# Score tiles of four levels for two token tiles in a gated linear attention, and its output with the state terms first

## The chip, the core and the metric

The kernel runs on one core of a Trainium2 chip. The time is the device time of one execution in microseconds (us). The engines work side by side, each through its own queue in order: TensorE (PE; its weight loads stand apart as PEld), VectorE (DVE), ScalarE (ACT), GpSimd (POOL), and SyncE (SP), whose queue issues the transfers from DRAM.

## The reference

The program is a block of two layers on 512 latent tokens and 256 context tokens, with 1024 features, and a second block behind it. In each layer three branches run side by side: a gated convolution, an attention and a gated linear attention (GLA). The GLA has four heads with 128 key and 256 value features. Its core, for one direction, is

```python
def _gla_scan(q, k, v, log_a, s0):
    ...
    def step(s, inp):
        qc, kc, vc, ac = inp
        bcum = jnp.cumsum(ac, axis=2)
        o_inter = jnp.einsum('bhtd,bhde->bhte', qc * jnp.exp(bcum), s)
        diff = bcum[:, :, :, None, :] - bcum[:, :, None, :, :]
        decay = jnp.exp(jnp.where(mask[:, :, None], diff, -jnp.inf))
        att = jnp.einsum('bhtd,bhsd,bhtsd->bhts', qc, kc, decay)
        o_intra = jnp.einsum('bhts,bhse->bhte', att, vc)
        b_last = bcum[:, :, -1:, :]
        s_new = jnp.exp(b_last[:, :, 0, :])[..., None] * s + jnp.einsum('bhsd,bhse->bhde', kc * jnp.exp(b_last - bcum), vc)
        return s_new, o_inter + o_intra
```

It runs over the tokens forward and backward, first over the context and from the states reached there over the latents; the two directions are added.

## The kernel before

The kernel works on tiles of 128 tokens. In such a tile the decay between two tokens depends on each feature, so the 128 x 128 square of scores is split into seven levels and a diagonal: at level L the tile falls into blocks of 128 >> L tokens, and the decay between a token of one half of a block and one of the other half is measured from the border between the halves. Each level is then a plain matmul of decayed queries with decayed keys, of which a 0/1 mask (`gm`, 8 x 128 columns) keeps the pairs that belong to that level. The eight masked squares are added into one.

`gla_levels` does this for one head. A *unit* is 256 tokens, two token tiles c = 0, 1. Per level, GpSimd makes four subtractions into a tile x (L946 to L949; the context's and the latents' x share three buffers), ScalarE takes the exponential (L950), VectorE multiplies by queries and keys (L951), and TensorE makes one score matmul for each c (L955). Both c have a score tile of 128 x 1024 columns, with a slot of 128 for each level and the diagonal (L959); there are two such buffers, `sc`. When the diagonal of c is done, VectorE masks its tile in two halves of four slots (L964), adds the four slots of each up (L968), and GpSimd adds the two sums into the square `att` (L973). Then the generator yields 1900.

`gla_out` makes the output of a head: for each of two blocks e of 128 value features, and each token tile i, the queries with the states of the two directions (`S`, forward and backward) and then the values with `att`, all by L994 into one bank `mm`, which has one buffer. ScalarE copies and squares the result.

`gla_main` calls for each head the states (`gla_states`), then the levels in turns with the decay of the next head (`gla_decay`, with the triangular matmul L854), then the output. This runs three times: on the context in layer 0 (one unit for each head), on the latents in layer 0 and on the latents in layer 1 (two units for each head); the context in layer 1 needs only states.

What sets the order around this is a pump. Other work of the layer, above all projections (L274, L276, with weights split in two parts by L253 on ScalarE and L254 on VectorE), is written as generators and put into a queue, the *filler*. Each yield of the GLA's generator names some nanoseconds; scaled (by 1.2 for the latents, 3.0 for the context) they buy that much filler, which is written behind it. Filler for the latents comes from projections, for the context at its end from the modulation: groups of four matmuls (L536) whose weights of 512 KB come by DMA into three buffers `wr`, with two groups of L548 to close. A scheduler then settles each engine's order. There is no filler when the queue is empty.

Of the kernel before, what the change touches and what calls it, by code (L numbers as in the profile page):

```python
# [10 lines left out]
F32 = mybir.dt.float32  # L11
# [3 lines left out]
ALU = mybir.AluOpType  # L15
# [169 lines left out]
class Kern:  # L185
# [745 lines left out]
    def gla_levels(self, G, hd):  # L931
# [3 lines left out]
        for un in range(T // 256):  # L935
            uc = slice(un * 256, (un + 1) * 256)
            sl = [self.sc() for _ in range(2)]
            for L in range(7):
# [13 lines left out]
                yield 1500  # L952
                for c in range(2):
                    cs = slice(c * 128, (c + 1) * 128)
                    nc.tensor.matmul(sl[c][:, L * 128:(L + 1) * 128], x[:, 1, cs], x[:, 0, cs],  # L955
                                     start=True, stop=True)
            for c in range(2):
                cs = slice(un * 256 + c * 128, un * 256 + (c + 1) * 128)
                nc.tensor.matmul(sl[c][:, 896:1024], qk[:, 1, cs], qk[:, 0, cs], start=True, stop=True)  # L959
                att = pool.tile([128, 128], F32, tag="att", name=self.nm("att"), bufs=4)  # L960
                part = None
                for hf in range(2):
                    pr = pool.tile([128, 512], F32, tag="pr", name=self.nm("pr"), bufs=1)
                    nc.vector.tensor_tensor(pr, sl[c][:, hf * 512:(hf + 1) * 512],  # L964
                                            G["gm"][:, 4 * hf:4 * hf + 4, :].rearrange("p a b -> p (a b)"),
                                            op=ALU.mult)
                    o = att if part is None else self.sm2()
                    nc.vector.tensor_reduce(o, pr.rearrange("p (a b) -> p b a", a=4),  # L968
                                            axis=mybir.AxisListType.X, op=ALU.add)
                    if part is None:  # L970
                        part = att
                    else:
                        nc.gpsimd.tensor_tensor(att, att, o, op=ALU.add)  # L973
                G["att"][hd].append(att)
                yield 1900
# [4 lines left out]
    def gla_out(self, G, hd, pump):  # L980
# [4 lines left out]
        for e in range(2):  # L985
# [4 lines left out]
            for i in range(nt):  # L990
                terms = [(S[d][i][:, es], qd[:, d, i * 128:(i + 1) * 128]) for d in range(2) if S[d][i] is not None]
                terms.append((gv[:, i, es], atts[i]))
                for n_, (a, b) in enumerate(terms):
# [1150 lines left out]
```

## Time and profile before

| | us |
|---|---|
| median of three runs | 3627.67 |
| lowest and highest | 3621.95 and 3629.71 |
| the profiled execution | 3630.32 |
| its span, first to last instruction | 3628.5 |
| TensorE busy | 3482.0 |
| VectorE busy | 2087.1 |
| ScalarE busy | 1502.2 |
| GpSimd busy | 457.7 |

The mean granted clock of TensorE is 0.985 of full speed. The span is shared between the instructions of the engines; busy times of different engines overlap, and only what TensorE doesn't do is left for a change that leaves its matmuls alone. A wait is named after the instruction that came last of those waited for. Each f32 matmul stands in the rows as two records (x2). The recorded time of a row with several records starts with the first and ends with the last, and overlaps the row behind it; the pace is read from start to start.

### The profile page before, as it was taken

Reading aid. Unit: us, or ns where it says so; the run is one execution under the profiler, and the core shown is the slowest. Engines: PE = TensorE matmul, PEld = TensorE weight load, DVE = VectorE, ACT = ScalarE, POOL = GpSimd, SP = SyncE. Lnnn points to the kernel's source line nnn. Section 1 sums busy time; section 2 is a strip of 40 time slices with the busy share of each in tenths; the row PEclk is TensorE's granted clock in tenths of the full one; section 3 lists DMA queues with packets and bytes.
Section 4 is the critical chain, followed back from the end, with each engine's and each line's share of the span. In section 5 each row is a group of like instructions: output and inputs, shape, how many; then the busy total and the mean of one; then the engine's idle time right before and its main releaser. Section 6 shows DMA issues by size and latency. Waiting matters only on the chain. (4 is left out here: it accounts for less than half of the span.)

```text
span 3628.5 us, 52736 instructions
## 1 busy us (share of the span) xinstructions
PE 3482.0 (96%) x20382; PEld 2966.3 (82%) x20382; DVE 2087.1 (58%) x4317; ACT 1502.2 (41%) x2574; POOL 457.7 (13%) x802
## 2 busy tenths in 40 slices
PE   7999999999999999999999999999899999989999
PEld 5998888988888878887888887887788687678887
DVE  5755556578545555666755555445576547665342
ACT  4543333445534434444553443222444445533241
POOL 0011211010123340010013332000200000000000
PEclk8999999999999999999999999999999999999999
DMA  6443334531222224532122222323412332232222
GB/s 226 133 145 115 117 119 150 199 112 47 73 83 73 80 92 154 180 124 85 53 72 79 74 85 88 116 99 128 164 59 79 103 107 86 77 110 87 95 99 93
DMA packets 144091, 386.61 MB, mean 107 GB/s; under 512 B 17496, under 2 KB 47456, under 8 KB 143584
## 3 DMA queue, kind: packets, MB, share of 16 engines
q1 hardware_dynamic: 143840, 383.24, 31.9%
q8 instruction: 160, 2.62, 0.3%
q14 instruction: 91, 0.75, 0.1%
HBM read 345.92 MB, written 30.96 MB: 104 GB/s over the span
## 5 line engine op out<-in xcount | busy, mean ns | idle before, releaser
L254 DVE TENSOR_TENSOR wl<-wr,wh 128x1024 fp32r<-128x1024 f32 x522 | 650.1, 1247 | 665.9 <-PE pj L274 325.3
L274 PE MATMUL pj<-h,wh 128*128 128x512 f32 (+1 forms) x2568 | 928.7, 372 | 13.9 <-ACT wh L253 5.5
L276 PE MATMUL pj<-h,wh 128*128 128x512 f32 (+1 forms) x2568 | 910.4, 365 | 0.0
L253 ACT ACTIVATE wh<-wr 128x1024 fp32r<-128x1024 f32 x522 | 550.3, 1057 | 778.1 <-PE pj L276 549.0
L274 PE MATMUL pj<-h,wl 128*128 128x512 f32 (+1 forms) x2568 | 594.2, 367 | 0.0
L274 PEld LDWEIGHTS pj<-h,wh 128*128 128x128 f32 x2568 | 488.6, 191 | 85.5 <-ACT wh L253 8.0
L276 PEld LDWEIGHTS pj<-h,wh 128*128 128x128 f32 x2568 | 488.7, 191 | 63.2 <-issue 0.6
L274 PEld LDWEIGHTS pj<-h,wl 128*128 128x128 f32 x2568 | 434.8, 190 | 68.1 <-issue 1.2
L274 PE MATMUL pj<-uh,wh 128*128 128x256 f32 (+1 forms) x1040 | 324.5, 335 | 17.0 <-ACT uh L258 5.1
L276 PE MATMUL pj<-ul,wh 128*128 128x256 f32 (+1 forms) x1040 | 320.6, 331 | 2.7 <-DVE ul L259 2.6
L274 PEld LDWEIGHTS pj<-uh,wh 128*128 128x128 f32 x1040 | 198.2, 191 | 37.8 <-ACT uh L258 6.5
L276 PEld LDWEIGHTS pj<-ul,wh 128*128 128x128 f32 x1040 | 199.2, 192 | 20.5 <-DVE ul L259 4.5
L274 PE MATMUL pj<-uh,wl 128*128 128x256 f32 (+1 forms) x1040 | 202.4, 333 | 0.0
L951 DVE TENSOR_TENSOR x<-x,qk 128x512 f32<-128x512 f32 x140 | 107.6, 774 | 133.9 <-ACT x L950 133.9
L950 ACT ACTIVATE x<-x 128x512 f32<-128x512 f32 x140 | 88.3, 631 | 230.5 <-POOL x L949 216.4
L320 PE MATMUL pj<-wh,h 128*128 128x256 f32 x608 | 176.7, 291 | 0.9 <-DVE vl L259 0.9
L322 PE MATMUL pj<-wl,h 128*128 128x256 f32 x608 | 174.2, 287 | 1.4 <-DVE wl L254 1.3
L274 PEld LDWEIGHTS pj<-uh,wl 128*128 128x128 f32 x1040 | 160.4, 194 | 15.7
L321 PE MATMUL pj<-wh,h 128*128 128x256 f32 x608 | 173.3, 285 | 0.0
L946 POOL TENSOR_TENSOR x<-bc 128x128 f32<-128x128 f32 x140 | 72.9, 521 | 466.8 <-PE sc L955 465.6
L322 PEld LDWEIGHTS pj<-wl,h 128*128 128x128 f32 x608 | 116.9, 192 | 2.4 <-DVE wl L254 2.0
L320 PEld LDWEIGHTS pj<-wh,h 128*128 128x128 f32 x608 | 117.2, 193 | 1.5 <-DVE vl L259 1.0
(376 smaller groups left out, 5887.6 us busy)
## 6 DMA issues: line engine op xcount, KB each, us to landing
wr<-in_w_br_dram SPq DMA_DIRECT2D x84, 512.0 KB
wr<-in_w_mg_dram SPq DMA_DIRECT2D x72, 512.0 KB
wr<-in_w_ada_dram SPq DMA_DIRECT2D x48, 512.0 KB
wr<-in_w_f_dram SPq DMA_DIRECT2D x45, 512.0 KB
wr<-in_w_o_dram SPq DMA_DIRECT2D x37, 512.0 KB
wr<-in_wt_gv_dram SPq DMA_DIRECT2D x32, 512.0 KB
wr<-in_w_up_dram SPq DMA_DIRECT2D x32, 512.0 KB
wr<-in_w_dn_dram SPq DMA_DIRECT2D x32, 512.0 KB
```

The lines of the kernel that those rows point to most:

```text
L253: self.nc.scalar.activation(hi, raw, AF.Copy)
L254: self.nc.vector.tensor_tensor(lo, raw, hi.bitcast(F32), op=ALU.subtract)
L274: t.matmul(ps[:, :T], c, h[k][0], start=start and n == k == 0, stop=stop and last)
L276: t.matmul(ps[:, :T], c, h[k][1], start=False, stop=False)
L320: t.matmul(ps[:, :256], hh, hi[:, c], start=k == 0, stop=False)
L321: t.matmul(ps[:, :256], hl, hi[:, c], start=False, stop=False)
L322: t.matmul(ps[:, :256], hh, lo[:, c], start=False, stop=k == KT - 1)
L946: nc.gpsimd.tensor_tensor(xv[0][:, :, 0, :], v[1][:, :, 0, :], cm, op=ALU.subtract)
L950: nc.scalar.activation(x, x, AF.Exp)
L951: nc.vector.tensor_tensor(x, x, qk[:, :, uc], op=ALU.mult)
```

## The change

A score tile now holds four levels of both token tiles: 512 columns for c = 0 and 512 for c = 1. The first tile of a unit takes levels 0 to 3, the second takes levels 4 to 6 and the diagonal. `masked(sl, hf)` masks one of them: for each c a product with the mask over 512 columns, a reduction, and for the second tile an addition to the first one's sum, on VectorE where GpSimd did it. It is called behind level 3 for the first tile and behind the diagonal for the second, and yields 1000 after each c, four times a unit where there were two yields of 1900. In the output, all state terms of a bank come first and all `att` terms last, with one start and one stop over the bank. Ahead of the output stands a new yield of 2500. In the changed code the mask's product is L943, the reduction L947, the addition L950, the level's product L966, the score matmul L973, the diagonal L978 and the output L998.

```diff
--- before.py
+++ after.py
@@ -934,7 +934,22 @@
         G["att"][hd] = []
         for un in range(T // 256):
             uc = slice(un * 256, (un + 1) * 256)
-            sl = [self.sc() for _ in range(2)]
+            att = [pool.tile([128, 128], F32, tag="att", name=self.nm("att"), bufs=4) for _ in range(2)]
+
+            def masked(sl, hf):
+
+                for c in range(2):
+                    pr = pool.tile([128, 512], F32, tag="pr", name=self.nm("pr"), bufs=1)
+                    nc.vector.tensor_tensor(pr, sl[:, c * 512:(c + 1) * 512],
+                                            G["gm"][:, 4 * hf:4 * hf + 4, :].rearrange("p a b -> p (a b)"),
+                                            op=ALU.mult)
+                    o = self.sm2() if hf else att[c]
+                    nc.vector.tensor_reduce(o, pr.rearrange("p (a b) -> p b a", a=4),
+                                            axis=mybir.AxisListType.X, op=ALU.add)
+                    if hf:
+                        nc.vector.tensor_tensor(att[c], att[c], o, op=ALU.add)
+                        G["att"][hd].append(att[c])
+                    yield 1000
             for L in range(7):
                 m = 64 >> L
                 x = pool.tile([128, 2, 256], F32, tag="x", name=self.nm("x"), bufs=3)
@@ -950,29 +965,18 @@
                 nc.scalar.activation(x, x, AF.Exp)
                 nc.vector.tensor_tensor(x, x, qk[:, :, uc], op=ALU.mult)
                 yield 1500
+                if L % 4 == 0:
+                    sl = self.sc()
                 for c in range(2):
                     cs = slice(c * 128, (c + 1) * 128)
-                    nc.tensor.matmul(sl[c][:, L * 128:(L + 1) * 128], x[:, 1, cs], x[:, 0, cs],
-                                     start=True, stop=True)
+                    os_ = slice(c * 512 + L % 4 * 128, c * 512 + L % 4 * 128 + 128)
+                    nc.tensor.matmul(sl[:, os_], x[:, 1, cs], x[:, 0, cs], start=True, stop=True)
+                if L == 3:
+                    yield from masked(sl, 0)
             for c in range(2):
                 cs = slice(un * 256 + c * 128, un * 256 + (c + 1) * 128)
-                nc.tensor.matmul(sl[c][:, 896:1024], qk[:, 1, cs], qk[:, 0, cs], start=True, stop=True)
-                att = pool.tile([128, 128], F32, tag="att", name=self.nm("att"), bufs=4)
-                part = None
-                for hf in range(2):
-                    pr = pool.tile([128, 512], F32, tag="pr", name=self.nm("pr"), bufs=1)
-                    nc.vector.tensor_tensor(pr, sl[c][:, hf * 512:(hf + 1) * 512],
-                                            G["gm"][:, 4 * hf:4 * hf + 4, :].rearrange("p a b -> p (a b)"),
-                                            op=ALU.mult)
-                    o = att if part is None else self.sm2()
-                    nc.vector.tensor_reduce(o, pr.rearrange("p (a b) -> p b a", a=4),
-                                            axis=mybir.AxisListType.X, op=ALU.add)
-                    if part is None:
-                        part = att
-                    else:
-                        nc.gpsimd.tensor_tensor(att, att, o, op=ALU.add)
-                G["att"][hd].append(att)
-                yield 1900
+                nc.tensor.matmul(sl[:, c * 512 + 384:c * 512 + 512], qk[:, 1, cs], qk[:, 0, cs], start=True, stop=True)
+            yield from masked(sl, 1)
 
     def sm2(self):
         return self.small.tile([128, 128], F32, tag="sp2", name=self.nm("sp2"), bufs=4)
@@ -987,11 +991,11 @@
             es = slice(e * 128, (e + 1) * 128)
             if e == 1:
                 G["ended"] = hd + 1
-            for i in range(nt):
-                terms = [(S[d][i][:, es], qd[:, d, i * 128:(i + 1) * 128]) for d in range(2) if S[d][i] is not None]
-                terms.append((gv[:, i, es], atts[i]))
-                for n_, (a, b) in enumerate(terms):
-                    nc.tensor.matmul(o[:, i * 128:(i + 1) * 128], a, b, start=n_ == 0, stop=n_ == len(terms) - 1)
+            terms = [(i, S[d][i][:, es], qd[:, d, i * 128:(i + 1) * 128])
+                     for i in range(nt) for d in range(2) if S[d][i] is not None]
+            terms += [(i, gv[:, i, es], atts[i]) for i in range(nt)]
+            for n_, (i, a, b) in enumerate(terms):
+                nc.tensor.matmul(o[:, i * 128:(i + 1) * 128], a, b, start=n_ == 0, stop=n_ == len(terms) - 1)
             ob = pool.tile([128, T], F32, tag="o", name=self.nm("o"), bufs=3)
             nc.scalar.activation(ob, o[:, :T], AF.Copy)
             sq = self.t()[:, :T]
@@ -1028,6 +1032,7 @@
                 G["used"] = hd + 1
                 if hd == 0:
                     yield from before_out
+                yield 2500
                 yield from self.gla_out(G, hd, pump)
             elif nxt:
                 G["used"] = hd + 1
```

The order of TensorE at the border between the two units of a head (latents, layer 1, head 2; the other heads are built alike). `sc` is a score tile, `x` the decayed pair of a level, `pj` a projection; the rows left out between are filler. Before, from the last level of unit 0 over its two diagonals to the first level of unit 1:

```order
L955 MATMUL sc_20759<-x_21041 128x128 [waits Pool_49]
L955 MATMUL sc_20760<-x_21041 128x128
L959 MATMUL sc_20759<-qk_20075 128x128
...
L959 MATMUL sc_20760<-qk_20075 128x128
...
L955 MATMUL sc_21112<-x_21114 128x128 [waits DVE_49,PE_49,Pool_49]
L955 MATMUL sc_21113<-x_21114 128x128 [waits DVE_49,PE_49]
```

After, at the same place:

```order
L973 MATMUL sc_21067<-x_21087 128x128 [waits DVE_49]
L973 MATMUL sc_21067<-x_21087 128x128
L978 MATMUL sc_21067<-qk_20076 128x128 x2
...
L973 MATMUL sc_21155<-x_21140 128x128 [waits DVE_49]
L973 MATMUL sc_21155<-x_21140 128x128
```

Twenty filler matmuls stand between the last diagonal and the first level in both. Before, both matmuls of the new unit wait for a tile that VectorE (and GpSimd and TensorE) must let go; after, they go into one tile and wait for VectorE alone, which makes `x` and has masked the tile's former content behind level 3.

The order of TensorE at the end of the last head (latents, layer 1, head 3). Before, from its last level to the output (`mm`), with filler in the gaps:

```order
L955 MATMUL sc_21723<-x_21851 128x128 [waits DVE_49]
L955 MATMUL sc_21724<-x_21851 128x128
L959 MATMUL sc_21723<-qk_20596 128x128
...
L959 MATMUL sc_21724<-qk_20596 128x128
L994 MATMUL mm_21899<-qd_21420,S_21415 128x128 [waits DMAHW4_49]
L994 MATMUL mm_21899<-qd_21420,S_21500 128x128
L994 MATMUL mm_21899<-att_21674,gv_20859 128x128
...
L994 MATMUL mm_21899<-att_21869,gv_20859 128x128 [waits Pool_49]
...
L994 MATMUL mm_21899<-att_21887,gv_20859 128x128 [waits Pool_49]
```

After, from level 3 on:

```order
L973 MATMUL sc_21786<-x_21833 128x128 [waits DVE_49]
L973 MATMUL sc_21786<-x_21833 128x128
L973 MATMUL sc_21866<-x_21859 128x128 [waits DVE_49]
L973 MATMUL sc_21866<-x_21859 128x128
L973 MATMUL sc_21866<-x_21869 128x128 [waits DVE_49]
L973 MATMUL sc_21866<-x_21869 128x128
L998 MATMUL mm_21899<-qd_21462,S_21457 128x128 [waits DMAHW6_49]
...
L973 MATMUL sc_21866<-x_21878 128x128 [waits DVE_49]
...
L978 MATMUL sc_21866<-qk_20562 128x128 x2
...
L998 MATMUL mm_21899<-att_21564,gv_20851 128x128
...
L998 MATMUL mm_21899<-att_21765,gv_20851 128x128 [waits DVE_49]
...
L998 MATMUL mm_21899<-att_21766,gv_20851 128x128 [waits DVE_49]
```

Before, eight filler matmuls stand between the levels to the end, eight between the diagonals, and two and ten ahead of the two `att` terms that wait. After, nothing stands between levels 3, 4 and 5; ahead of level 6 are six state terms; and behind the first two `att` terms come nine fillers, an `att` term, six fillers and the last.

The order of TensorE at the end of the context (layer 0, head 3). L536 and L548 are the modulation, L854 is the triangular matmul of a head's decay, and rows left out are parts of the same groups and other levels. Before:

```order
L854 MATMUL mm_5842<-tril,la_5498 128x128 [waits DVE_49]
...
L536 MATMUL pj_5959<-wr_5957,sil_98 32x256 [waits DMAHW5_49,DVE_49]
L536 MATMUL pj_5959<-wr_5957,sil_98 32x256 x3
L955 MATMUL sc_6201<-x_6203 128x128 [waits Pool_49]
L955 MATMUL sc_6202<-x_6203 128x128
...
L536 MATMUL pj_5967<-wr_5965,sil_98 32x256 [waits DMAHW6_49,DVE_49]
...
L536 MATMUL pj_5975<-wr_5973,sil_98 32x256 [waits DMAHW7_49,DVE_49]
...
L955 MATMUL sc_6201<-x_6230 128x128 [waits DVE_49]
...
L536 MATMUL pj_5990<-wr_5988,sil_98 32x256 [waits DMAHW1_49,PE_49]
...
L955 MATMUL sc_6201<-x_6239 128x128 [waits DVE_49]
...
L536 MATMUL pj_6018<-wr_6016,sil_98 32x256 [waits DMAHW4_49,Activation_49]
...
L536 MATMUL pj_6026<-wr_6024,sil_98 32x256 [waits DMAHW5_49,DVE_49]
```

After:

```order
L536 MATMUL pj_5926<-wr_5924,sil_98 32x256 [waits DMAHW5_49,DVE_49]
...
L536 MATMUL pj_5934<-wr_5932,sil_98 32x256 [waits DMAHW6_49,DVE_49]
...
L536 MATMUL pj_5942<-wr_5940,sil_98 32x256 [waits DMAHW7_49,DVE_49]
...
L548 MATMUL mm_5953<-sel,acc_5834 128x2 [waits DVE_49,Activation_49]
...
L536 MATMUL pj_5962<-wr_5960,sil_98 32x256 [waits DMAHW1_49,PE_49]
...
L536 MATMUL pj_5970<-wr_5968,sil_98 32x256 [waits DMAHW2_49,PE_49]
...
L536 MATMUL pj_5978<-wr_5976,sil_98 32x256 [waits DMAHW4_49,Activation_49]
...
L536 MATMUL pj_5986<-wr_5984,sil_98 32x256 [waits DMAHW5_49,DVE_49]
...
L548 MATMUL mm_5992<-sel,acc_5959 128x2 [waits DVE_49]
...
L854 MATMUL mm_6000<-tril,la_5635 128x128 [waits DVE_49]
...
L998 MATMUL mm_6050<-qd_5325,S_5471 128x128 [waits Activation_49]
```

Before, the seven modulation groups lie between the levels of head 3, and that head's L854 stands earlier. After, they stand one behind the other, the L854 behind them, and then the output of head 2 (L998) and the levels of head 3 further on.

## Rows read from the trace of the kernel before

**Rows 1.** The page: busy time, share and instructions of each engine.

```profile
PE 3482.0 (96%) x20382; PEld 2966.3 (82%) x20382; DVE 2087.1 (58%) x4317; ACT 1502.2 (41%) x2574; POOL 457.7 (13%) x802
```

**Rows 2.** TensorE's waits: waiter, releaser: us in total, times, longest.

```profile
PE sc L955 <- DVE pr L964: 16.4, 8, 2.5
PE mm L994 <- POOL att L973: 16.3, 10, 3.0
```

**Rows 3.** Timeline, TensorE, layer 0, heads 2, 3: start, us, ..., [idle before].

```profile
1268.92 0.46 PE L955 MATMUL sc<-x 128*128 128x128 f32 x2 [2.54 <-DVE pr L964]
...
1294.56 0.49 PE L994 MATMUL mm<-att,gv 128*128 128x128 f32 x2 [3.00 <-POOL att L973]
...
1368.47 0.49 PE L994 MATMUL mm<-att,gv 128*128 128x128 f32 x2 [0.91 <-POOL att L973]
...
1372.19 0.49 PE L994 MATMUL mm<-att,gv 128*128 128x128 f32 x2 [0.46 <-POOL att L973]
```

**Rows 4.** Windows, TensorE: us, busy, granted clock, DMA share, GB/s.

```profile
1292.00:1296.00 4.00, 1.44 (x6) 0.93 0.38 131
1296.00:1300.00 4.00, 4.00 (x23) 0.64 0.21 65
```

**Rows 5.** Groups by form: operation, count | busy us, mean ns | idle before.

```profile
L964 DVE TENSOR_TENSOR pr<-sc,gm 128x512 f32<-128x512 f32 x80 | 55.0, 688 | 14.7 <-PE sc L959 12.4
...
L968 DVE TENSOR_REDUCE att<-pr 128x128 f32<-128x512 f32 x40 | 42.4, 1060 | 1.2
...
L973 POOL TENSOR_TENSOR att<-att,sp 128x128 f32<-128x128 f32 x40 | 22.1, 552 | 151.2 <-DVE sp L968 151.2
```

**Rows 6.** One tile's instructions: an addition, ns least/median/most.

```profile
L821 DVE TENSOR_TENSOR o<-o,f x24: 418/684/915, 363.2 to 2272.4; 128x512 f32<-128x512 f32 x16, 128x256 f32<-128x256 f32 x8
```

**Rows 7.** Timeline, TensorE: the pace of filler, levels and output.

```profile
1270.84 0.40 PE L276 MATMUL pj<-h,wh 128*128 128x512 f32 x1
1271.08 0.60 PE L955 MATMUL sc<-x 128*128 128x128 f32 x4
1271.44 0.48 PE L274 MATMUL pj<-h,wh 128*128 128x512 f32 x1
...
1288.94 0.61 PE L994 MATMUL mm<-qd,S 128*128 128x128 f32 x4
1289.38 0.39 PE L994 MATMUL mm<-att,gv 128*128 128x128 f32 x2
```

**Rows 8.** Timeline, ScalarE, GpSimd and VectorE, at a level of head 2.

```profile
1273.90 0.63 ACT L950 ACTIVATE x<-x 128x512 f32<-128x512 f32 x1 [1.94 <-POOL x L949]
...
1274.46 0.40 POOL L947 TENSOR_TENSOR x<-bc 128x128 f32<-128x128 f32 x1
...
1274.56 0.84 DVE L951 TENSOR_TENSOR x<-x,qk 128x512 f32<-128x512 f32 x1 [1.73 <-ACT x L950]
...
1274.82 0.85 POOL L948 TENSOR_TENSOR x<-bc 128x128 f32<-128x128 f32 x1
```

**Rows 9.** Timeline, TensorE: the context's last head.

```profile
575.16 0.71 PE L955 MATMUL sc<-x 128*128 128x128 f32 x4 [1.07 <-DVE x L951]
...
576.59 0.64 PE L536 MATMUL pj<-wr,sil 128*32 128x256 f32 x8
...
580.91 0.71 PE L955 MATMUL sc<-x 128*128 128x128 f32 x4 [0.37 <-DVE x L951]
...
586.02 1.87 PE L548 MATMUL mm<-sel,acc 128*128 128x2 f32 x8 [2.95 <-DVE acc L544]
```

**Rows 10.** Timeline, SyncE: loads of the modulation's weights issued.

```profile
571.08 1.76 SPq L244 DMA_DIRECT2D wr<-in_w_ada_dram  x2
```

**Rows 11.** Windows, all engines, 572 to 592 us: us, busy, clock, DMA, GB/s.

```profile
584.00:588.00 4.00, 1.87 (x8) 1.78 (x8) 2.64 (x6) 0.98 (x1) 0.45 (x1) 0.69 0.62 243
588.00:592.00 4.00, 3.85 (x18) 3.86 (x19) 4.00 (x8) 1.60 (x3) 0.02 (x1) 0.50 0.03 10
sum 20.00, PE 14.03 PEld 10.77 DVE 14.05 ACT 5.45 POOL 7.94; mean PE 2.81 PEld 2.15 DVE 2.81 ACT 1.09 POOL 1.59
```

## The prediction

> **What bounds the kernel now.** I began with the busy times of the page: TensorE works 3482.0 of 3628.5 us [rows 1], so a change can shorten only its idle 146.5 us, its slow-clock stretches, or its own instructions. The number of score, diagonal and output matmuls stays as it is, so TensorE's own work does not change. Next came the list of what TensorE waits for [rows 2]. Two entries belong to the code that is changed: the first score matmul of a unit waits for VectorE's mask of the unit before (16.4 us in 8 waits), and the output matmul waits for the last partial sum of a score square, made on GpSimd (16.3 us in 10 waits). Then the timeline gave the single stalls [rows 3]: in head 2 of layer 0, 2.54 us at the unit boundary and 3.00 us at the output, in head 3 0.91 and 0.46 us at the output. The pattern repeats in both layers: one boundary for each of eight heads makes the 8 waits. Last, the granted clock around the 3.00 us stall [rows 4]: 0.93 in the 4 us that hold it and 0.64 in the next 4, in which TensorE is busy throughout. Between its two levels, 1.2 and 2.4 GHz, that loses 0.07 x 4 + 0.36 x 4 = 1.7 us of full speed.
>
> **The change, term by term**, against the profiled execution's own 3630.3 us (its span plus what lies around it; the median of the three runs is 2.6 us lower).
>
> A. Unit boundary. Before, both score tiles of a unit are written to the last slot before the masks begin, and the next unit's first score matmul waits until VectorE has let them go. VectorE needs 0.69 us for a masking product and 1.06 us for a reduction [rows 5], so the two masks of one tile hold it 2 x (0.69 + 1.06) = 3.5 us, and four take 7.0; the filler behind the diagonal is 20 matmuls of 0.24 us [rows 7], 4.8 us. After, the next unit takes the tile that held levels 0 to 3, which is masked three levels earlier, at some 2.3 us a level (8 fillers and one pair of 0.36 us, [rows 7]). Three levels are 6.8 us against a mask of 3.5. The order shows that the wait on it has gone, and only the wait for the level's own product is left, which VectorE holds ahead of the second mask. Two units' waits in four heads and two layers: **-16.4 us**. What can be late instead is the product of level 0 itself, as in the context, where it costs 1.07 and 0.37 us [rows 9]; it is made before the mask, so I count nothing.
>
> B. Output. Behind the diagonal VectorE had four masks and reductions and GpSimd one addition of 0.55 us [rows 5]: 7.0 + 0.55 = 7.55 us. Now only two halves remain there, with an addition on VectorE. The trace has no such addition of 128 columns on VectorE. The nearest rows are a two-input addition at 0.42 us for 256 and 0.68 for 512 columns [rows 6]; halving the step (0.13) again below gives 0.28. The tail is 2 x (0.69 + 1.06 + 0.28) = 4.06 us, 3.5 less, and the cover for heads 0 to 2 (24 filler matmuls) is as long as before. The longest wait is 3.0, so these go. Of the 16.3 us, 2 x 1.37 = 2.7 are the last heads' (C); the other 13.6 us go, except for 1 us. That remainder is for the new addition's uncertain end. A GpSimd subtraction takes 0.40 us alone and 0.85 beside VectorE's product [rows 8], so GpSimd is held by such a product, and an addition may be held in turn by a subtraction of 0.40: 0.68 instead of 0.28 for each, tail 4.9 us, 0.35 us left of each 3.0 us wait. Term: **-12.5 us** (-13.5 to -11).
>
> The Trainium skill speaks against moving an addition to VectorE here: by "SBUF — State Buffer", section "SBUF: two separate sides", a VectorE instruction with two SBUF inputs and a GpSimd instruction that reads SBUF exclude each other for a whole instruction. The trace agrees (0.40 against 0.85, [rows 8]). If the rule held for every addition the term would be about -12 instead of -13.5, and the sum -17.5 instead of -19; since the subtractions are delayed by 2 x 0.28 us a unit, while GpSimd loses 2 x 0.55 us of its own, it sets no new pace.
>
> C. Tail of the last head. Head 3 has no next head to take filler from, and the changed order spends it three levels earlier: the new yields in the loop buy projections there. Between levels 4 and 5 there is none, and levels 5, 6 and the diagonal have only eight output matmuls. Counted from the matmuls of level 3: level 6 waits for the slot of level 3, then four subtractions (some 2 us, two of them slowed), exponential (0.63) and product (0.84) [rows 8], 3.5 us; VectorE then has the rest of the first mask (2.8 us) and the second (4.06), so the last score square is ready after 10.4 us. TensorE's work up to there is four pairs (levels 4 to 6, diagonal) of 0.36 us, ten output matmuls of 0.22 and 15 fillers of 0.24 [rows 7], 7.3 us. So 3.1 us of stall, and with one weight conversion in VectorE's queue between, 4.4; I take 4.5 for each layer against 1.37 before (0.91 + 0.46 [rows 3]), **+6.3 us**. If the products run ahead it is 0, if two conversions and a held exponential stand between, +14.
>
> D. Clock. Stalls of over 2 us at boundary and output go, some two episodes in each layer at 1.7 us [rows 4]: -6.8. If the tails of C make one each, +3.4 comes back. I take **-3.4** (-6.8 to +3.4).
>
> E. Tail of the context. The same yields stand in the context's attention, whose filler is the modulation: seven groups of matmuls (L536) whose weights come by DMA through three buffers, with two L548 groups. Before, they stand between the levels of head 3, so that loads and levels hide each other: between 572 and 592 us TensorE works 14.03 of 20 [rows 11] (a load is issued at 571.08 [rows 10] and the group that needs it is at 576.59 or before [rows 9]). After, the seven stand bare, ahead of the state matmul L854 of head 3, on which all its levels hang. Price of a bare group: from nothing (landed) to the 5.5 us between those two rows; I take 4 us for a load whose buffer is freed just before. Groups 1 to 3 have theirs, 4 to 6 come 4 us after 1, and 7 another 4 us later: 11 us for 4 us of work, 7 idle. The levels of head 3 then run at GpSimd's pace, three from 575.16 to 580.91 [rows 9], 1.92 us each against 0.36 of work; some three of them have no cover, 5 idle. Together 12 against 6.0 before, +6.3 with the accumulation wait of 2.95 us [rows 9] kept. The clock is at 0.69 and 0.50 [rows 11] in 8 us before, 3.2 us lost; a longer bare stretch adds some 1.7. **+8 us** (+2 to +16).
>
> Sum: -16.4 - 12.5 + 6.3 - 3.4 + 8 = **-18.0 us**, 3612.3 for an execution like the profiled one, and 3627.7 - 18.0 = **3610** for the median.
>
> **The rivals.**
> R1, slower. The bare stretches cost more than the stalls they replace: C at +14, clock +3.4, E at +16, against -28.9: +4.5, some 3632. It decides if C, D and E together exceed 29 us. For it: E's ladder is made of loads, and one load delayed by others delays four groups; against it: the ladder starts with three loads landed.
> R2, a larger gain. VectorE runs ahead in the tails and the loads have landed: C 0, D -6.8, E +2, B -13.5, A -16.4: -34.7, 3593. For it: the levels' products need no filler themselves; against it: there is no filler left between levels 4 and 6.
> R3, half the gain. The output's wait stays, since VectorE works its queue in order, and between product and reduction of the second mask stands the next head's level product, which waits for ScalarE. Then B is half, -6, and a low-clock episode for each layer stays (+3.4): -18 + 6.5 + 3.4 = -8, 3620 (3618 to 3626). For it: that chain takes 3.5 us for a level; against: the cover of 24 fillers is unchanged and the tail 3.5 us shorter.
> R4, the change does not do what it says: the first mask is queued behind products that wait for levels 4 to 6, so the tile is late and A stays: -1.6, 3626. Against it stands the order of VectorE, in which the first mask comes right behind level 3.
>
> **How the numbers follow.** Forecast (3600 to 3618) 0.58, R2 0.17, R3 0.13, R4 0.04, R1 0.08. About 0.2% (7.3 us) is what a measurement of this kernel can tell from no change, so faster means below 3620.4: forecast less 0.03 for its upper edge, R2, and 0.04 of R3, 0.76. Slower means above 3635 and takes 0.06 of R1, whose upper end lies beyond its middle. The rest is 0.18. The range 3594 to 3623 leaves out R1 (0.08), R4 (0.04), the upper third of R3 (0.04) and the lower end of R2 (0.04).
>
> **What would show it.** A: the wait of the score matmul for the mask is absent from the list, at most 2 us remain. B: the output's waits in heads 0 to 2 are at most 0.5 us each. C: stalls of 3 to 6 us in all in the last head of each layer, at the levels and the output. D: full clock at the unit boundaries; a low stretch, if any, behind the last head. E: in the context's tail L536 waits for its weights some 7 us, and the levels for the product. The prediction is wrong if the output's wait stays above 8 us (R3), if the bare stretches of the tails cost over 29 us (R1), or if TensorE's idle falls by more than 30 us (R2).

## The result, and where the time went

The changed kernel takes 3583.68 us (median of four runs, 3581.93 to 3588.62) against 3626.38 us before: a ratio of 0.9893, 95% interval 0.9881 to 0.9905. That is 42.7 us less, where 18 were forecast. The profiled execution has a span of 3586.8 us. One execution among all of this document ran in a slow state (6826.06 us, of the version with the mask written behind the diagonal); the ratios leave it out.

The page of the changed kernel, busy time of each engine (compare [rows 1]):

```profile
PE 3468.3 (97%) x20382; PEld 2955.6 (82%) x20382; DVE 2093.8 (58%) x4357; ACT 1503.6 (42%) x2574; POOL 440.2 (12%) x762
```

TensorE's idle time fell from 146.5 to 118.5 us, and although it has the same 20382 instructions, its busy time fell by 13.7 us too: an instruction at a low clock counts as a longer one (a filler matmul of 0.40 us [rows 7] takes 0.63 at 1296.07, where the clock is 0.64 [rows 4]).

To see where this happened, the program is cut at five instructions at which both kernels have done the same work. The columns are the stretch in us, its length, TensorE's busy time (instructions), the granted clock, DMA share and GB/s; the stretches are the context of layer 0 from its middle on, the latents' attention of layer 0, what lies between, the latents' attention of layer 1, and the rest. Before:

```profile
451.30:975.00 523.70, 506.63 (x3389) 0.99 0.36 120
975.00:1400.40 425.40, 404.17 (x2239) 0.98 0.26 86
1400.40:1870.10 469.70, 452.23 (x2786) 0.98 0.35 112
1870.10:2284.50 414.40, 393.47 (x2195) 0.99 0.26 85
2284.50:3628.50 1344.00, 1302.80 (x6783) 0.99 0.30 99
```

After:

```profile
451.00:982.50 531.50, 511.02 (x3387) 0.97 0.36 117
982.50:1386.40 403.90, 396.64 (x2238) 1.00 0.28 93
1386.40:1851.20 464.80, 449.05 (x2785) 0.99 0.35 111
1851.20:2243.40 392.20, 386.64 (x2194) 1.00 0.27 89
2243.40:3586.80 1343.40, 1302.64 (x6783) 0.99 0.30 99
```

The context's stretch loses 7.8 us, the latents' two gain 21.5 and 22.2, together 43.7. What lies between them gains 4.9, 3.2 of it in TensorE's busy time. In the fourteen profiles of the experiments, three of them of versions of the kernel before, its length runs from 462.5 to 467.9 us, with the edits and without them; so I give that part to no step. The rest is equal. In the latents' stretches TensorE's idle is 21.2 and 20.9 us before, 7.3 and 5.6 after: 29.3 us of the 43.7. The remaining 14.4 stand in its busy time.

The list of TensorE's waits after (waiter, releaser: us in total, times, longest), which answers [rows 2]:

```profile
PE sc L973 <- DVE x L966: 6.8, 7, 1.4
...
PE mm L998 <- DVE att L950: 2.0, 4, 0.8
```

No score matmul waits for a mask any more (16.4 us before), and of the output's 16.3 us 2.0 are left, all of it in the last heads. Their end in layer 0, with the idle time in brackets (compare the last two of [rows 3]):

```profile
1346.74 0.71 PE L973 MATMUL sc<-x 128*128 128x128 f32 x4 [0.98 <-DVE x L966]
...
1349.73 0.71 PE L973 MATMUL sc<-x 128*128 128x128 f32 x4 [0.93 <-DVE x L966]
...
1354.69 0.49 PE L998 MATMUL mm<-att,gv 128*128 128x128 f32 x2 [0.83 <-DVE att L950]
...
1356.72 0.49 PE L998 MATMUL mm<-att,gv 128*128 128x128 f32 x2 [0.15 <-DVE att L950]
```

That is 2.9 us where 4.5 were forecast and 1.37 stood before; layer 1 has the same four rows 859 us later.

The clock of the kernel before, in windows of 5 us around every low stretch that lies in the latents' two attentions (columns as above):

```profile
1199.00:1204.00 5.00, 5.00 (x25) 0.66 0.21 72
1233.00:1238.00 5.00, 4.95 (x21) 0.66 0.00 0
1295.00:1300.00 5.00, 5.00 (x27) 0.66 0.18 55
1346.00:1351.00 5.00, 4.64 (x17) 0.66 0.24 92
2117.00:2122.00 5.00, 4.83 (x20) 0.66 0.01 3
2179.00:2184.00 5.00, 5.00 (x26) 0.66 0.20 52
2230.00:2235.00 5.00, 4.71 (x17) 0.66 0.21 84
```

There are seven, at 0.34 x 5 = 1.7 us each, 11.9 us. I had counted four. Each stands right behind a stall of 1.5 to 3.0 us: at the output (2.26, 3.00, and 3.00 in layer 1), at the unit boundary (2.39 in both layers), and twice at the transposition L839 of the next head's decay (1.50), a wait that the forecast did not count at all. Timeline before, layer 0:

```profile
1198.82 0.49 PE L994 MATMUL mm<-att,gv 128*128 128x128 f32 x2 [2.26 <-POOL att L973]
...
1233.05 1.20 PE L839 MATMUL tr<-wd,rT 65*128 65x128 f32 x8 [1.50 <-ACT la L843]
```

Not every stall has one: the 2.54 us at 1268.92 [rows 3] is followed by none, and neither is its like in layer 1. After, both stretches stand at 1.00 but for their first microsecond, which is the end of a low stretch of the context (0.5 us). So 11.4 us of clock come back. In this execution the tails of the last heads bring none:

```profile
1348.00:1352.00 4.00, 3.07 (x26) 1.00 0.12 35
1352.00:1356.00 4.00, 3.17 (x16) 1.00 0.02 4
```

In the context's tail the seven modulation groups stand bare, as forecast. Timeline of TensorE, after (compare [rows 9]):

```profile
572.26 1.08 PE L536 MATMUL pj<-wr,sil 128*32 128x256 f32 x8 [2.14 <-DMA wr<-in_w_ada_dram]
...
595.71 0.71 PE L973 MATMUL sc<-x 128*128 128x128 f32 x4 [1.31 <-DVE x L966]
```

TensorE's waits in the whole of the context's stretch, after:

```profile
PE pj L536 <- DMA wr<-in_w_ada_dram: 4.3, 3, 2.1
PE sc L973 <- DVE x L966: 2.9, 3, 1.4
...
PE tr L839 <- DMA S<-sd: 2.2, 1, 2.2
```

And the clock in the tail, all of it at the lower level (compare [rows 11]):

```profile
572.00:576.00 4.00, 1.81 (x16) 0.50 0.89 316
...
580.00:584.00 4.00, 3.74 (x17) 0.50 0.56 205
```

### The profile page after: what moved, and what is told of

Same layout as the page of the kernel before. It is cut to its first block, busy times and chain, and to the rows that moved or that the text cites. A ratio compares the mean times of both kernels' runs of the same rounds, so it can differ in the third digit from the quotient of the medians.

```text
span 3586.8 us, 52744 instructions
## 1 busy us (share of the span) xinstructions
PE 3468.3 (97%) x20382; PEld 2955.6 (82%) x20382; DVE 2093.8 (58%) x4357; ACT 1503.6 (42%) x2574; POOL 440.2 (12%) x762
## 5 line engine op out<-in xcount | busy, mean ns | idle before, releaser
L274 PE MATMUL pj<-h,wl 128*128 128x512 f32 (+1 forms) x2568 | 585.8, 365 | 0.0
L966 DVE TENSOR_TENSOR x<-x,qk 128x512 f32<-128x512 f32 x140 | 104.9, 755 | 117.7 <-ACT x L965 117.5
```

The costliest lines, as they stand in the source:

```text
L274: t.matmul(ps[:, :T], c, h[k][0], start=start and n == k == 0, stop=stop and last)
L966: nc.vector.tensor_tensor(x, x, qk[:, :, uc], op=ALU.mult)
```

## The experiments

Two questions were put to the chip: which part of the change carries the gain, and what a stall costs. Theory: the early mask and the grouping by levels take the stalls away, and with them goes more than their waits. Rival: the amount and the place of the filler, or the addition's engine, or the output's order, does it.

**The mask written behind the diagonal.** The first mask stands behind the diagonal in the text, all else as changed.

```diff
                 if L == 3:
-                    yield from masked(sl, 0)
+                    first = sl
+                    yield 1000
+                    yield 1000
...
+            for _ in masked(first, 0):
+                pass
             yield from masked(sl, 1)
```

> The changed kernel, but both masks of a unit stand behind its diagonal, as before the change; tiles, yields and the order of TensorE are those of the changed kernel. Theory 1 (the early mask is what frees the tile and shortens the tail): the waits at the unit boundary come back at 1.6 to 2.5 us, those at the output at 1.5 to 3.0 us, with the low-clock stretches: +35 to +45 us against the changed kernel, about 3624. Theory 2 (grouping a tile by levels is enough at the boundary, since the next unit needs only the tile that is masked first, 3.5 us against 4.8 us of filler; the early mask counts only at the output): boundary waits of at most 0.5 us each, output waits of 1 to 2.5 us in heads 0 to 2, +10 to +20 us. Theory 3 (only the amount of filler counts): within 5 us of the changed kernel.

3589.24 us, ratio 0.9900 (0.9880 to 0.9919). None of the theories was tested: the scheduler put the mask back behind level 3, as the order of VectorE shows, and the last head has the same four stalls (0.98, 0.93, 0.85, 0.15). It is a repetition of the changed kernel, in another build. What settles when a mask runs is what it reads, so the next version changes that.

**A first tile that is full late.** The first tile takes levels 0, 1, 2 and 6, so that its mask can't run before level 6; both masks are called behind the diagonal, and the table of the masks is loaded in the new order. Filler and the order of TensorE are the changed kernel's.

```diff
-                if L % 4 == 0:
-                    sl = self.sc()
+                if L == 0:
+                    ta = self.sc()
+                if L == 3:
+                    tb = self.sc()
+                sl, slot = (ta, L if L < 3 else 3) if L in (0, 1, 2, 6) else (tb, L - 3)
...
```

> The changed kernel with other levels in its two score tiles: the first takes levels 0, 1, 2 and 6, the second 3, 4, 5 and the diagonal, so that the first mask can't begin before level 6 and VectorE has 7 to 7.6 us behind the diagonal again. Filler and the order of TensorE are those of the changed kernel. Theory 1 (the early mask carries the gain): boundary waits of 1.5 us or more, output waits of 1.5 to 3 us with low-clock stretches: +15 to +45 us against the changed kernel. Theory 2 (the amount of filler at the output and a tile that is let go after two masks are enough): boundary waits of at most 0.5 us, output waits of at most 1.5 us: within 8 us of the changed kernel.

3616.63 us, ratio 0.9982 (0.9973 to 0.9991): 33 us of the gain are gone. The latents' stretches take 417.2 and 409.4 us. Waits of TensorE:

```profile
PE mm L1004 <- DVE att L950: 10.4, 13, 1.5
PE sc L976 <- DVE x L966: 9.0, 9, 1.5
PE sc L976 <- DVE pr L943: 8.9, 8, 1.8
```

Theory 1 holds for the time (15 to 45 us more), with waits of half the forecast size and more of them, and with low clock in few places (1.00 and 0.99 over the two stretches): the first tile is let go after two masks, and the boundary costs 8.9 us where it cost 16.4.

**The early mask in the former tiles.** The kernel before, with its first halves masked behind level 3, and nothing else.

```diff
+                if L == 3:
+                    for c in range(2):
+                        atts.append(pool.tile([128, 128], F32, tag="att", name=self.nm("att"), bufs=4))
+                        half(c, 0)
...
```

> The kernel before with one part of the change alone: the first half of each score tile (levels 0 to 3) is masked behind level 3. Tiles for each token tile, yields, output order and the addition on GpSimd stay as before, and nothing is changed in the context's filler. Theory 1 (the early mask carries the gain): the boundary waits and the output waits of heads 0 to 2 go with their low-clock stretches: 3580 to 3600 us, and the context's tail stays as before. Theory 2 (it needs tiles by level, or the new yield): boundary or output waits of over 1 us each stay, 3610 to 3627 us.

3604.46 us, ratio 0.9947 (0.9932 to 0.9962), just above theory 1. The latents' stretches take 414.2 and 404.8 us. The waits at the boundary and at the output of heads 0 to 2 are gone. What is left stands in one line of the waits, 16.2 us, and the timeline shows where:

```profile
PE sc L967 <- DVE pr L942: 16.2, 18, 1.5
```

```profile
1087.79 0.46 PE L967 MATMUL sc<-x 128*128 128x128 f32 x2 [0.29 <-POOL x L961]
1090.54 0.49 PE L967 MATMUL sc<-x 128*128 128x128 f32 x2 [1.14 <-DVE pr L942]
```

These are the two matmuls of level 4, in the middle of a unit; most of the 18 places are of this kind. The second must wait until the mask of the first half has read the same score tile. So the early mask trades the wait at the boundary for one at level 4, and the grouping by levels gives level 4 a tile of its own.

**Both, and nothing else.** Tiles by level and the early mask; the addition on GpSimd, the former output order, no yield of 2500, four yields of 950. Against the changed kernel:

```diff
-                        nc.vector.tensor_tensor(att[c], att[c], o, op=ALU.add)
+                        nc.gpsimd.tensor_tensor(att[c], att[c], o, op=ALU.add)
...
-                    yield 1000
+                    yield 950
...
-                yield 2500
                 yield from self.gla_out(G, hd, pump)
```

> The kernel before with tiles by level and the early mask alone: the addition is on GpSimd, the output has its former order, there is no yield of 2500, and the four yields of a unit are 950 each, which is the former sum. Against the run with the early mask in the former tiles this adds only the grouping by level. Theory 1 (early mask and grouping work together, since in the former tiles the matmuls of level 4 wait until the first half of the same tile is read; the rest of the change is worth nothing): 3572 to 3584 us, no waits of level 4 for the mask. Theory 2 (the rest, the addition on VectorE, the yield and the output order, carries some of it): 3590 to 3605 us.

3593.67 us, ratio 0.9909 (0.9894 to 0.9923), in the range of theory 2 (3590 to 3605): the rest carries some of it. No score matmul waits for a mask. Not only the grouping is new against the version before it, though: two of the four yields now stand behind level 3, and their filler could hide the wait of level 4 as well. No run parts the two. The trace of the changed kernel, which has the same filler there and more, speaks for the grouping (TensorE and VectorE, layer 1, head 2, level 4):

```profile
2134.48 0.61 PE L973 MATMUL sc<-x 128*128 128x128 f32 x4
```

```profile
2136.39 0.69 DVE L943 TENSOR_TENSOR pr<-sc,gm 128x512 f32<-128x512 f32 x1
```

The matmul of level 4 runs 1.9 us ahead of the mask of the second token tile's first half. In a shared tile it would have had to wait for it, as in the version before; this is argued from the trace, not run.

The latents' stretches take 409.0 and 398.9 us, 31.9 us less than before and 11.8 more than changed; the waits of the output are 10.3 us in 10 places, up to 1.5 each. The rest of the change, with yields of 1000 for 950, covers these.

**The rest, one part at a time.** Each of the three is the changed kernel with one part undone: `nc.gpsimd` for the addition, the yield of 2500 taken out, the output's terms token tile by token tile.

> The changed kernel with the addition of the two halves on GpSimd again, 40 of 0.55 us. Theory 1 (the engine of the addition is indifferent: the tail is 2 x 1.75 + 0.55 = 4.05 us on GpSimd against 2 x 2.03 = 4.06 us on VectorE): within 4 us of the changed kernel, no output wait over 0.8 us in heads 0 to 2. Theory 2 (GpSimd's queue holds the addition behind the next head's subtractions, some 2 us): output waits of 0.5 to 2 us in six heads, +5 to +20 us.

> The changed kernel without the new yield of 2500 ahead of the output: 12 fillers instead of 24 stand between the last diagonal and the output in heads 0 to 2, and the filler lasts longer at the ends. Theory 1 (the yield is not needed: 12 x 0.24 + 10 x 0.22 = 5.1 us against 4.1 us of VectorE's tail): output waits of at most 0.5 us, the context's tail and the last heads gain 2 to 6 us, 3577 to 3583. Theory 2 (the yield is what hides the tail): output waits of 1 to 2 us in six heads with low-clock stretches, +8 to +25 us.

> The changed kernel with the output's terms in their former order, token tile by token tile. The first square that is waited for is needed two matmuls (0.44 us) earlier. Theory 1 (the order of the terms is indifferent, the tail is 4.1 us against 24 fillers of 0.24 us and the terms): within 3 us of the changed kernel. Theory 2 (states first is what hides the tail): output waits of 0.5 us or more in each head, +8 us or more.

With GpSimd's addition 3587.09 us (ratio 0.9895, 0.9881 to 0.9910), without the yield 3578.49 (0.9871, 0.9856 to 0.9885), with the former output order 3584.10 (0.9889, 0.9873 to 0.9905). The latents' stretches take 799.8, 799.7 and 796.4 us together, against 796.1. So none of the three is worth more than 3.7 us alone, while all three together are worth 11.8: they cover the same last 1 to 2 us at the output, and any two of them nearly do. Without the yield the waits of the output come to 7.7 us, so theory 1 there was right on the time (3577 to 3583) and wrong on the cover; the context's stretch is 13.6 us shorter:

```profile
450.00:967.90 517.90, 505.23 (x3388) 0.99 0.36 121
```

**Filler alone.** The kernel before with the yield of 2500 alone, and then with more filler at both places, in the latents alone:

```diff
-                yield 1900
+                yield 4500 if T > 256 and c == 1 else 1900
...
+                if G["T"] > 256:
+                    yield 2500
                 yield from self.gla_out(G, hd, pump)
```

> The kernel before with the new yield of 2500 ahead of the output alone: some 12 more fillers of 0.24 us stand behind the last diagonal. Theory 1 (filler hides the output waits as well as a shorter tail does): the output waits of heads 0 to 2 go (-13.6 us and half of the low-clock stretches), the boundary waits of 16.4 us stay, and the context's tail has its modulation bare as in the changed kernel (+5 to +8): 3605 to 3620 us. Theory 2 (the output waits follow VectorE's queue, not the filler): 3625 to 3640 us.

> The kernel before with more filler in the latents alone: 4500 instead of 1900 behind a unit's last mask, and 2500 ahead of the output. Masks, tiles, the addition and the output order stay as before, and the context is not touched. Theory 1 (the gain is the stalls, by whatever means they are hidden): boundary and output waits of heads 0 to 2 go with their low-clock stretches, the latents' two stretches take 800 to 812 us in all instead of 839.8, and only the last heads, whose filler ends earlier, keep some of it: 3588 to 3602 us. Theory 2 (the shorter work of the masks behind the diagonal is what counts): 3612 us or more.

The first takes 3618.23 us (0.9987, 0.9977 to 0.9997), in the range of its theory 1: the output's waits fall from 16.3 to 7.0 us, the boundary's stay at 18.3, and the context pays (531.8 us against 523.7). The second takes 3630.18 us (1.0009, 0.9998 to 1.0019), and its latents' stretches are not shorter, 426.7 and 419.1 us. The number of its theory 2 came, but not for its reason. Heads 0 to 2 are covered (boundary waits of at most 0.8 us), but the filler is used up before the second unit of head 3, and there everything stands bare:

```profile
1353.03 0.91 PE L955 MATMUL sc<-x 128*128 128x128 f32 x6 [3.79 <-DVE pr L964]
...
1361.12 0.49 PE L994 MATMUL mm<-att,gv 128*128 128x128 f32 x2 [2.07 <-POOL att L973]
```

Filler is a sum that is spent once: it moves a stall to the end of the queue. A shorter tail removes it.

**The price of a stall.** The changed kernel with 10 or 24 copies of 128 x 128 on VectorE (0.23 us each) ahead of the last addition of heads 0 to 2.

```diff
                     if hf:
+                        if T > 256 and un == 1 and hd < 3 and c == 1:
+                            for _ in range(10):
+                                nc.vector.tensor_copy(o, o)
                         nc.vector.tensor_tensor(att[c], att[c], o, op=ALU.add)
```

> The changed kernel with ten copies of 128 x 128 on VectorE between the last reduction and the last addition of heads 0 to 2 of the latents, six places, some 2 to 3 us each against a slack of about 1.5 us. It prices a stall of TensorE. Theory 1 (a stall costs its wait plus some 0.17 us of lost overlap, and 1.7 us of clock only where it is long): output waits of 0.5 to 1.5 us, time up by their sum plus some 1 us. Theory 2 (every stall brings a low-clock stretch): sum of the waits plus 6 x 1.9 us.

> The same with 24 copies, 5 to 7 us at each of the six places; the order puts twelve more fillers ahead of the last term, so that stalls of 2 to 4 us are left. Theory 1 (long stalls bring a low-clock stretch of 1.7 us and 0.17 us of overlap each): time up by 1.4 to 2 times the sum of the added waits. Theory 2 (a stall costs its wait alone, and the low stretches of the kernel before have another cause): time up by the sum of the waits within 3 us.

3596.26 us (0.9925, 0.9909 to 0.9942) and 3607.69 us (0.9949, 0.9934 to 0.9964). The latents' stretches with 10 and with 24 copies:

```profile
978.70:1387.80 409.10, 397.66 (x2239) 1.00 0.27 91
1852.60:2251.70 399.10, 388.53 (x2196) 1.00 0.26 88
```

```profile
979.10:1394.40 415.30, 400.10 (x2238) 0.99 0.26 91
1859.80:2263.10 403.30, 389.79 (x2195) 1.00 0.26 88
```

Idle rises from 12.8 to 22.0 and 28.7 us (length less busy time), by 9.2 and 15.9; the stretches grow by 12.1 and 22.5. So a microsecond of stall costs 1.3 and 1.4 us, and in the change itself 43.7 / 29.3 = 1.5. With 10 copies there is one low stretch in each layer, behind the stall of 2.52 us in head 2, 3.4 us in all:

```profile
1291.00:1296.00 5.00, 4.79 (x22) 0.66 0.04 12
2155.00:2160.00 5.00, 4.30 (x20) 0.66 0.00 0
```

Less the 0.5 us of the changed kernel's own they make the whole of what is paid beyond the waits, 12.1 - 9.2 = 2.9. With 24 copies the stall of 3.41 us in head 2 of layer 0 is followed by a low stretch, the one of 2.98 us in head 1 by none; in layer 1 it is the other way round (2.98 with, 3.43 without). Layer 0:

```profile
1199.00:1204.00 5.00, 3.04 (x15) 1.00 0.20 79
1205.00:1210.00 5.00, 4.98 (x35) 1.00 0.41 143
1298.00:1303.00 5.00, 5.00 (x24) 0.66 0.38 126
```

Theory 1 is the nearer with 10 copies (10.2 us by its sum, 20.6 by theory 2's) and holds with 24 for the ratio at its lower edge; that every long stall brings a low stretch does not hold.

**The context.** Three versions of the changed kernel take the yield of 2500 out of the context: with four yields of 950 there, which is the former sum; the same with less filler spent early in the latents' last head; and with nothing else changed:

```diff
-                yield 2500
+                if G["T"] > 256:
+                    yield 2500
                 yield from self.gla_out(G, hd, pump)
```

> The changed kernel with the former amount of yields in the context alone (four of 950 a unit, no 2500 ahead of the output); the modulation groups stand between the levels of the context's last head again. Theory 1 (the bare modulation costs what the traces show between 560 and 1000 us): 4 to 9 us less than the changed kernel, 3575 to 3580 us. Theory 2 (loads and levels only change places): within 3 us of the changed kernel.

> The changed kernel with the context's yields at their former amount, and in the last head of the latents no yield of 2500 and four of 500, so that filler lasts two levels longer. Theory 1 (what the bare stretches cost is had back): 3572 to 3580 us. Theory 2 (the last head's tail is set by VectorE's queue, whatever the filler): as with the context's yields alone, 3578 to 3582 us.

> The changed kernel without the yield of 2500 in the context; all else stays. Theory 1 (that yield alone makes the modulation stand bare ahead of the last head): the context's stretch takes 517 to 525 us instead of 531.5, the latents' stretches stay at 796: 3570 to 3578 us. Theory 2 (the mask's four yields of 1000 do it as well): 3580 us or more.

3579.92 us (0.9883, 0.9869 to 0.9898), 3580.15 us (0.9873, 0.9859 to 0.9888) and 3568.70 us (0.9857, 0.9837 to 0.9876). The second has the same stalls in its last heads, moved (1.09, 1.47, 0.38), so that tail follows VectorE's queue and not the filler. In the third the modulation stands between the levels of head 3 again. The context's stretch in the first and in the third:

```profile
453.40:977.90 524.50, 506.19 (x3388) 0.99 0.35 119
```

```profile
450.80:969.40 518.60, 506.71 (x3388) 0.99 0.36 121
```

The third is the fastest of all, 15 us below the changed kernel (13 by the ratios), with a context of 518.6 us against 531.5. The first has no yield of 2500 there either, but its context takes 524.5 us, as long as before, and by its ratio it can't be told from the changed kernel. So two things are at work. The yield of 2500 costs the context 8 to 13 us: with it, the changed kernel's context takes 531.5 us in its own profile and 527 in those of the two doses, whose edits stand in the latents alone; without it 518.6, and 517.9 in the version without any yield of 2500. And four yields of 1000 in place of 950 save it 6 us, all of it idle time (18.3 us against 11.9). Why so small a shift of filler does that, no run shows.

## Why the prediction was right or wrong

The direction and the places of the stalls were right; the size was not, and the time lies below the range. The step that failed is D, the clock, with two waits that were not counted. The sign that was named for a larger gain, TensorE's idle falling by more than 30 us, did not come (28.0): the surplus stands in the busy time. By its steps:

- A, the unit boundary, -16.4: measured as forecast, the wait is off the list. The reason given was only half of it. Masking early is not enough: in the former tiles it puts the wait at level 4, 16.2 us in all. The tile by levels gives the next level a free tile.
- B, the output, -12.5: -13.6. The addition on VectorE takes 276 to 547 ns, median 292, against the 0.28 that was worked out from the wider ones. The hold by GpSimd's subtractions, for which up to 1 us was to stay, shows at most in the two longest (0.52 and 0.55 us, both beside a subtraction; six others that overlap one take 0.29) and costs nothing at the output. The tail was worked out as masks and additions alone; before, VectorE also had a level product of the next head (0.68 us) and a weight conversion (1.21 us) between them, and the last mask began 5.9 us behind its diagonal (2176.18 and 2170.28, layer 1, head 2).
- C, the last heads, +6.3: +3.0, or 2.9 us in each layer. The chain worked out without a weight conversion, 3.1 us, was the better one; I had put one in.
- D, the clock, -3.4: -11.4 (seven low stretches of 1.7 us before, 0.5 us left). This is the step that failed most. I multiplied one stall's low stretch by a guess of two in each layer, where a row for each of seven stood in the same trace, and then gave half back for tails that brought none. That they brought none does not hold for every version: in the one with GpSimd's addition, tails of 1.24, 1.16 and 0.43 us bring one in each layer (1350 to 1355 and 2210 to 2215, clock 0.66).
- Two terms were missing. Waits that came behind the stalls went with them: the fillers' wait for ScalarE's conversion (0.94 us in each layer) and the wait of L839 (1.50 us, now 0.54). That is 3.8 us; less 1.6 us more of waiting for transfers behind the last head (L774), it makes some 29.3 of the 16.4 + 13.6 - 3.0 = 27.0. And 29.3 of idle and 11.4 of clock leave 3.0 us of the 43.7, whose cause stays open. Lost overlap at a stall may be one: a filler of 0.40 us is followed by the next after 0.23 [rows 7], and ahead of a stall this 0.17 is not had. Twelve waits fewer (30 before, 18 after, in the two stretches) would make 2.0; this is an estimate, and no run isolates it.
- E, the context, +8: +7.8. The sum was met by luck, its parts were not. Forecast were 6.3 us of idle (12 against 6.0 make 6.0) and 1.7 of clock; measured are 3.4 us of idle (17.1 before, 20.5 after) and 4.4 of busy time. The weights cost 4.3 us where 7 were forecast, the levels' waits 2.9 as against 2.8 before, and 2.2 us are a wait for a transfer of the states (L839) that the forecast did not name. Other profiles of the same context give 527 us, +3. And the yield's own price, 8 to 13 us, is in part hidden by the 6 us that the yields of 1000 save.

A to D came to -26.0, and the stretches they stand in gave -43.7; E's sum was met. The rival of a larger gain, 3593, named two of the right signs (tails that cost little, all of the clock had back), but not the amount, and had the context at +2. Half the gain (R3) did not happen: the output's wait is gone, with the next head's product in VectorE's queue.

## What to carry to other kernels

Price a stall of the bounding engine by more than its wait: here 1.3 to 1.5 us for each microsecond, most of the surplus in low stretches of the clock, which can't be counted on at any one stall. List every low stretch of the clock and every small wait behind the stall before multiplying one of them. Where masks or reductions close a stage, lay the tile out so that what is finished first is in a buffer that the next stage's writes do not touch; doing the work early in a shared tile moves a part of the wait (16.2 us here). And filler from a queue that runs empty hides a stall in one place by baring another, so ask at each new place that spends it who had it before.

## What the runs showed of the hardware

A low stretch of the clock (0.66 over 5 us) follows a stall of 1.5 to 3.4 us often but not always, and the length of the stall alone does not decide it. Before, there are seven in the latents' attentions: behind 1.50 us in both layers, and behind 2.54 us in neither. With 24 copies there is one behind 3.41 us and none behind 2.98 in layer 0, and one behind 2.98 and none behind 3.43 in layer 1. Tails of 2.9 us in four pieces brought none in the changed kernel, tails of 2.8 us in three pieces one each with GpSimd's addition. VectorE's additions of two SBUF operands took 276 ns at the least and 547 at the most for the same 128 columns.
